# Moving every on-chip pool of a two-layer decoder trunk by 32 bytes

## The chip, the core and the metric

The kernel is one program on one core of a Trainium2 chip. The metric is the device time of that program in microseconds; the comparison is between two programs that compute the same thing from the same inputs. On-chip memory (SBUF) is 128 partitions wide; a tile takes the same byte range in each of them, so an address below is a byte offset within a partition.

## What is computed

A decoder of two layers on 512 tokens of width 1024, all in 4-byte floats. Layer 0 mixes with a gated delta rule (6 heads of 128, worked out in chunks), layer 1 with sliding-window attention (12 query heads, 2 key/value heads); both also attend to 256 memory tokens. After each mixer comes an output product and a gated feed-forward part of width 2816, at the end a norm.

```python
def swiglu(h, w_gate_up, w_down):
    gu = h @ w_gate_up
    return (jax.nn.silu(gu[..., :D_FF]) * gu[..., D_FF:]) @ w_down
...
    for layer in range(DEPTH):
        h = rms_norm(x, ln_mix[layer])
        ...
        x = x + jnp.concatenate([mix_out.astype(x.dtype), mem_o.astype(x.dtype)], axis=-1) @ w_out[layer]
        x = x + swiglu(rms_norm(x, ln_ffn[layer]), w_gate_up[layer], w_down[layer])
    return rms_norm(x, ln_final)
```

Nearly all of the work is in the products with weights: the mixers' input and output products, the two feed-forward parts and the memory keys and values.

## The kernel before

Activations lie transposed: eight tiles of 128 rows (channels) by 512 columns (tokens). A weight arrives by DMA as a raw 128 x 1024 tile (`wraw`); ScalarE copies it to a rounded type (`whi`, type fp32r), VectorE subtracts and keeps the rest (`wlo`). Activations are split in the same way into pairs (`h` and `l`, in the feed-forward part's second half `ac8h` to `ac10l`). A product (`mm3`, called by `project`, `row`, `product` and others) is then three matmuls for each 128 x 128 block: `whi` with the high part, `whi` with the low part, `wlo` with the high part. Line 146 issues all of them; each one also loads its 128 x 128 weights (PEld). Called fp32r matmuls here, they come in two sizes: 512 columns (`pj` tiles most of the time) and 256 columns.

The matmuls with 256 columns come from the feed-forward part: there pairs of gate or up tiles are multiplied by a scheme that saves one block product in eight (`quarters`, `token_sums`); the moving operand is a half of a tile pair `T` (sums of token blocks) or a half of `h` and `l`, the stationary one a half of `whi`/`wlo`. Other matmuls (attention scores, transposes, the delta rule's chunk products, the norm's sums) are in plain float32.

Memory is given out by pools. Pools opened on the left stand one after another upwards from the constants, and stay: `const`, `w` (raw and split weights), `acta`, later `actb` and `x`. Pools with `side="right"` stand downwards from the top, and are opened and closed by stage (`layer0`, `early`, `gdn`, `ffn0`, `swa`, `ffn1`). Each tile's size is rounded up to 32 bytes. `const` holds 3128, 516, 96 and 8 bytes per partition; with the rounding it ends at byte 20320. Here is where the built program puts things:

| operand | pool, side | bytes from a multiple of 128 |
|---|---|---|
| `whi`, `wlo`, `wraw` | w, left | 96 |
| `h`, `l` | acta and actb, left | 96 |
| `x`, `rstd`, `sqa` | x, left | 96 |
| `T`, `ac8h` to `ac10l`, `mh`, `ml`, `mq0h` to `mq1l` | right | 96 |
| other right-hand tiles (`ws`, `fg`, `kn`, `sm`, ...) | right | 0, 32, 64 or 96 |

So of the 6,070 fp32r matmuls 6,042 have both operands at 96; of the rest, 16 (`sc<-h,wabs`, `sc<-l,wabs`) have the moving operand at 96 and the weights at 0, and 12 at the start, on zeros, both at 0.

The order of instructions on each engine follows the order of the calls; a few added dependencies (`nosync`) hold it. TensorE's queue has no DMA issues in it; weights are fetched from SyncE's queue, and the accumulating loads of `quarters` from GpSimd's.

Of the kernel before, what the change touches and what calls it, by code (L numbers as in the profile page):

```python
# [9 lines left out]
F32 = mybir.dt.float32  # L10
# [8 lines left out]
P = 128  # L19
# [67 lines left out]
class Builder:  # L87
# [146 lines left out]
    def build(self):  # L234
        tc, nc, a = self.tc, self.nc, self.a
        with ExitStack() as st:
            opened = lambda name, **kw: tc.tile_pool(name=name, bufs=1, reuse_waits="tile", **kw)
            pool = lambda name, **kw: st.enter_context(opened(name, **kw))
            cp = pool("const")
            self.wpool, self.apool = pool("w"), pool("acta")  # L240
            self.dpool = pool("scratch", space=DRAM)
            self.load_constants(cp)
            self.weng = nc.vector
            with opened("layer0", side="right") as self.mpool:
                with self.banks(pj=3, g=2, sc=3):
                    with opened("early", side="right") as ep:
                        self.mem_and_norm(ep)
                    with opened("gdn", side="right") as gp:
                        mix = self.gdn(gp)
                    self.bpool, xp = pool("actb"), pool("x")  # L250
                    self.x = [self.t(xp, [P, T], F32, f"x{k}") for k in range(KD)]
                    for k in range(KD):
                        nc.sync.dma_start(self.x[k], a["xT"][:, k, :])
                    self.rstd, self.cosT, self.sinT = (self.t(xp, [P, T], F32, n) for n in ("rstd", "cosT", "sinT"))
                    h = self.output(xp, 0, mix)
            with opened("ffn0", side="right") as fp, self.banks(pj=2, g=6):
                self.ffn(fp, xp, 0, h, self.apool, rope=True)
            with self.banks(pj=2, qk=2, pt=2), opened("swa", side="right") as sp:
                h = self.output(xp, 1, *self.swa(sp))
            with opened("ffn1", side="right") as fp, self.banks(pj=2, g=6):  # L260
                self.ffn(fp, xp, 1, h, self.bpool)
# [1154 lines left out]
```

## Time and profile before

| | |
|---|---|
| time, median of 3 runs | 1157.3 us (1157.09 to 1158.04) |
| span of the profiled execution | 1155.8 us |
| mean granted TensorE clock | 0.997 |
| instructions | 19296 |

The profile was taken on one execution of the same program; its span, from the first to the last instruction, is 1.5 us below the median of the timed runs. In its rows a matmul's duration runs from its start to its modelled end, with the time that results take to come out, so durations of neighbours overlap. The pace of a stream is the distance between starts; it is read from the timeline, or from a piece of the chain of waits as its length divided by its count.

### The profile page before, as it was taken

How to read it: one execution, taken by the hardware profiler on the slowest of the kernel's cores; microseconds unless marked ns; L12 is line 12 of the kernel's file. 1: busy time of each engine (PE TensorE's matmuls, PEld its weight loads, DVE VectorE, ACT ScalarE, POOL GpSimd, SP SyncE). 2: the span in 40 equal slices, each digit the busy share in tenths (PEclk: the TensorE clock that was granted, in tenths of full speed). 3: DMA queues.
4: the chain of work that ended last, by engine and by line, in shares of the span. 5: the costliest groups of instructions: out<-in, count | busy, mean ns of one | idle time of the engine just before them, and what ended most of it. 6: DMA issues, size and time to landing. Idle time of an engine off the chain costs nothing.

```text
span 1155.8 us, 19296 instructions
## 1 busy us (share of the span) xinstructions
PE 1142.6 (99%) x7342; PEld 997.1 (86%) x7342; DVE 834.0 (72%) x1559; ACT 626.7 (54%) x1249; POOL 86.0 (7%) x97
## 2 busy tenths in 40 slices
PE   9999999999999999999999999999999999999996
PEld 7788777877899998899998877788899988999886
DVE  5664886767889877488965777839989644889554
ACT  6489672366566642266653554856666412666433
POOL 0230000000101101011100000001111000111000
PEclk9999999999999999999999999999999999999998
DMA  8244341225657636367623421117577533676232
GB/s 314 84 150 116 131 119 66 95 88 164 188 128 182 169 103 168 114 168 187 154 82 99 124 72 42 51 56 200 131 181 184 151 96 107 170 185 153 78 98 85
DMA packets 72559, 151.20 MB, mean 131 GB/s; under 512 B 16732, under 2 KB 18932, under 8 KB 72468
## 3 DMA queue, kind: packets, MB, share of 16 engines
q1 hardware_dynamic: 61060, 129.28, 35.9%
q0 software_dynamic: 11136, 20.45, 11.2%
q8 instruction: 57, 0.93, 0.3%
q14 instruction: 34, 0.28, 0.1%
q10 hardware_dynamic: 272, 0.26, 0.1%
HBM read 143.00 MB, written 6.96 MB: 130 GB/s over the span
## 4 chain that ended last, share of the span: by engine, by line
PE 93%; DVE 3%; ACT 2%; DMA 1%; issue 0%; SPq 0%; DVEq 0%; ACTq 0%
PE pj L146 43%; PE g L146 38%; PE sc L146 6%; PE qk L146 3%; PE pt L146 2%; PE pt L150 1%; PE g L150 1%; DMA wraw<-in_wmk 1%; ACT sm L134 1%; DVE qv L156 1%; DVE big L153 0%; DVE wlo L153 0%; ACT T L140 0%; DVE btmp L153 0%; DMA wraw<-in_wdn 0%
## 5 line engine op out<-in xcount | busy, mean ns | idle before, releaser
L140 ACT ACTIVATE whi<-wraw 128x512 fp32r<-128x512 f32 (+3 forms) x324 | 240.9, 750 | 254.5 <-PE pj L146 159.2
L153 DVE TENSOR_TENSOR wlo<-wraw,whi 128x512 fp32r<-128x512 f32 (+3 forms) x324 | 270.4, 844 | 100.7 <-ACT whi L140 95.2
L146 PE MATMUL pj<-h,whi 128*128 128x512 f32 (+1 forms) x652 | 257.4, 396 | 0.0
L146 PE MATMUL pj<-l,whi 128*128 128x512 f32 (+1 forms) x652 | 255.0, 392 | 0.0
L146 PE MATMUL pj<-h,wlo 128*128 128x512 f32 (+1 forms) x652 | 254.1, 391 | 0.0
L146 PE MATMUL g<-T,whi 128*128 128x256 f32 x1216 | 220.6, 282 | 0.8 <-ACT fs L140 0.8
L146 PEld LDWEIGHTS g<-T,whi 128*128 128x128 f32 x1216 | 186.9, 189 | 2.1 <-DVE fu L156 1.1
L146 PE MATMUL g<-T,wlo 128*128 128x256 f32 x608 | 171.1, 281 | 0.0
L146 PEld LDWEIGHTS pj<-h,whi 128*128 128x128 f32 x652 | 122.4, 188 | 28.6 <-issue 3.6
L146 PE MATMUL g<-h,whi 128*128 128x256 f32 (+1 forms) x500 | 146.5, 293 | 0.0
L146 PE MATMUL g<-h,wlo 128*128 128x256 f32 (+1 forms) x500 | 145.8, 292 | 0.0
L146 PE MATMUL g<-l,whi 128*128 128x256 f32 (+1 forms) x500 | 145.5, 291 | 0.0
L146 PEld LDWEIGHTS pj<-h,wlo 128*128 128x128 f32 x652 | 122.5, 188 | 25.3 <-issue 0.6
L146 PEld LDWEIGHTS pj<-l,whi 128*128 128x128 f32 x652 | 122.6, 188 | 25.2 <-issue 1.1
L146 PEld LDWEIGHTS g<-T,wlo 128*128 128x128 f32 x608 | 114.4, 188 | 0.0
L146 PEld LDWEIGHTS g<-h,whi 128*128 128x128 f32 x500 | 95.0, 190 | 2.3 <-issue 0.5
L146 PEld LDWEIGHTS g<-l,whi 128*128 128x128 f32 x500 | 94.9, 190 | 2.3 <-issue 0.5
L146 PEld LDWEIGHTS g<-h,wlo 128*128 128x128 f32 x500 | 95.0, 190 | 1.7
L1125 POOL DMA_DIRECT2D ws<-in_wgu x38 | 33.3, 875 | 712.5 <-ACT h L140 447.7
L140 ACT ACTIVATE whi<-ws 128x512 fp32r<-128x512 f32 x76 | 48.0, 631 | 49.1 <-PE g L146 41.4
L153 DVE TENSOR_TENSOR fu<-pj,rstd 128x512 f32<-128x512 f32 (+1 forms) x34 | 22.4, 660 | 53.7 <-PE pj L146 53.7
L153 DVE TENSOR_TENSOR wlo<-ws,whi 128x512 fp32r<-128x512 f32 x76 | 52.2, 687 | 7.4 <-ACT whi L140 7.2
(381 smaller groups left out, 1701.1 us busy)
## 6 DMA issues: line engine op xcount, KB each, us to landing
wraw<-in_wgu SPq DMA_DIRECT2D x50, 512.0 KB, 4.2
ws<-in_wgu SPq DMA_DIRECT2D x76, 256.0 KB, 3.6
ws<-in_wgu POOLq DMA_DIRECT2D x76, 256.0 KB, 4.7
wraw<-in_win SPq DMA_DIRECT2D x26, 512.0 KB, 3.6
wraw<-in_wdn SPq DMA_DIRECT2D x32, 384.0 KB, 3.1
wraw<-in_wdn SPq DMA_DIRECT2D x32, 320.0 KB, 3.0
wraw<-in_wgu SPq DMA_DIRECT2D x38, 256.0 KB, 4.3
wraw<-in_wout SPq DMA_DIRECT2D x16, 512.0 KB, 3.6
```

The source lines that it names most:

```text
L134: ins = self.nc.scalar.activation(out, in_, func, **kw).ins
L140: self.copied = self.nc.scalar.activation(out, in_, AF.Copy, **kw).ins
L146: return self.nc.tensor.matmul(out, lhsT, rhs, start=start, stop=stop, skip_group_check=more).ins
L150: return self.nc.tensor.transpose(out, in_, self.ident[:k, :k]).ins
L153: return eng.tensor_tensor(out=out, in0=a, in1=b, op=op).ins
L156: return self.nc.vector.scalar_tensor_tensor(out=out, in0=in0, scalar=scalar, in1=in1, op0=op0, op1=op1).ins
L1125: nc.gpsimd.dma_start(s1, a22, accum_op=ALU.add)
```

## The change

Two tiles of 8 floats (32 bytes) are added that nothing reads or writes, one in a pool behind `const` on the left, and one in a pool opened first on the right.

```diff
             cp = pool("const")
+            self.t(pool("edge"), [P, 8], F32, "edge")
+            self.t(pool("far", side="right"), [P, 8], F32, "far")
             self.wpool, self.apool = pool("w"), pool("acta")
```

Left of it only the constants stay where they were. All other left-hand tiles move up by 32 bytes, all right-hand tiles down by 32. Every engine has the same instructions in the same order with the same waits. The built program's placement of the fp32r matmuls' operands (bytes from a multiple of 128) becomes:

| columns | moving operand | weights | matmuls |
|---|---|---|---|
| 512 | 0 | 0 | 2160 |
| 512 | 0 | 64 (48), 96 (16) | 64 |
| 512 | 64 | 0 | 318 |
| 512 | 96 | 96 (on zeros, at the start) | 12 |
| 256 | 0 | 0 (1416), 64 (144) | 1560 |
| 256 | 64 | 0 (1938), 64 (18) | 1956 |

Right-hand tiles that were at 64 from a multiple of 128 are at 32 now, and those at 0 at 96. Between a left-hand and a right-hand tile the distance is 64 bytes smaller than before.

## The prediction

> **What bounds the kernel now.** I read the page's first two parts, then the chain of waits, then TensorE's own waits, and last the timeline of TensorE inside the chain's longest pieces.
>
> ```profile
> PE 1142.6 (99%) x7342; PEld 997.1 (86%) x7342; DVE 834.0 (72%) x1559; ACT 626.7 (54%) x1249; POOL 86.0 (7%) x97
> PE 93%; DVE 3%; ACT 2%; DMA 1%; issue 0%; SPq 0%; DVEq 0%; ACTq 0%
> PE g L146 <- POOL wabs L366: 1.3, 1, 1.3
> 422.88 65.29 PE pj L146 x285
> 488.16 103.91 PE g L146 x852
> 332.19 88.48 PE g L146 x744
> ```
>
> The first row is the page's busy time, the second its chain, the third the longest entry of TensorE's waits, the last three are pieces of the chain. The reader is to see that TensorE does not wait for anybody: its longest wait in the whole run is 1.3 us, and 93% of the chain that sets the end is its own work. So the time moves when the pace of its matmuls moves, and hardly by anything else. The chain's pieces give that pace: 65.29 / 285 = 229 ns for a stream with mostly 512 columns, 88.48 / 744 = 118.9 ns for one with 256 columns. Now the same at close range, as start, length and count on the timeline:
>
> ```profile
> 460.55 0.40 PE L146 MATMUL pj<-h,whi 128*128 128x512 f32 x1
> ...
> 463.28 0.39 PE L146 MATMUL pj<-h,whi 128*128 128x512 f32 x1
> ...
> 17.22 0.28 PE L146 MATMUL pj<-whi,mh 128*128 128x256 f32 x1
> ...
> 17.82 0.28 PE L146 MATMUL pj<-wlo,mh 128*128 128x256 f32 x1
> ```
>
> From 460.55 to 463.28 there are twelve steps with no gap: 2.73 / 12 = 227.5 ns for 512 columns. The 256-column rows from 17.22 to 17.82 are five steps of 0.12 us, and the long pieces say 118.9 ns. The difference of 256 columns costs 227.5 - 118.9 = 108.6 ns, or 0.424 ns a column. Take the columns away and the same rest is left on both sizes: 227.5 - 512 x 0.424 = 10.4 ns, 118.9 - 256 x 0.424 = 10.4 ns. A rest that does not grow with the size is paid once for each matmul. In columns it is 10.4 / 0.424 = 24.5, which in 4-byte floats is 98 bytes. That is the size of a piece of memory that is read at the start without being needed: with every moving operand at 96 bytes past a multiple of 128 (and 32 past a multiple of 64), a reader that fetches 64 or 128 bytes at a time would need one fetch more than the data has. The rest lies between one such piece of 64 bytes (16 columns, 6.8 ns) and one of 128 (32 columns, 13.6 ns).
>
> **The change, part by part.** It removes and adds no instruction, DMA or wait, and every engine's order is the same. So all of its effect is in how long instructions take at their new addresses. Three kinds have to be looked at.
>
> ScalarE, VectorE and DMAs: nothing. ScalarE's copies of the same size from two places show it:
>
> ```profile
> L140 ACT ACTIVATE whi<-wraw 128x512 fp32r<-128x512 f32 x194 | 120.2, 629 | 70.1 <-PE g L146 49.0 <-PE pj L146 17.3 <-DVE wraw L153 1.8
> L140 ACT ACTIVATE whi<-ws 128x512 fp32r<-128x512 f32 x76 | 48.0, 631 | 49.1 <-PE g L146 41.4 <-ACT fs L140 7.8
> L153 DVE TENSOR_TENSOR wlo<-wraw,whi 128x512 fp32r<-128x512 f32 x194 | 131.1, 690 | 19.8 <-ACT whi L140 14.6
> L153 DVE TENSOR_TENSOR wlo<-ws,whi 128x512 fp32r<-128x512 f32 x76 | 52.2, 687 | 7.4 <-ACT whi L140 7.2
> ```
>
> `wraw` lies at 96, `ws` in most rows at 64: 629 against 631 ns, 690 against 687. Were they to change after all, it is TensorE that hides them (DVE is busy 72%, ACT 54%), and these engines do not end any long wait of TensorE. The transfers are hidden in the same way; a DMA sets 1% of the chain.
>
> Plain float32 matmuls: nothing. The scores of layer 1 give a clean pair, the moving tile `ks` at 0 and `mk` at 96:
>
> ```profile
> L146 PE MATMUL qk<-ks,q x96: 272/376/378, 692.3 to 745.6; 64*128 64x256 f32 x72, 64*128 64x128 f32 x24
> L146 PE MATMUL qk<-mk,q x32: 376/376/480, 665.8 to 680.5; 64*128 64x256 f32 x32
> 16.00 1.03 PE L146 MATMUL g<-sq,consts 128*128 128x256 f32 x4
> ```
>
> Both have a median of 376 ns, so 96 bytes cost plain float32 nothing. But that does not settle it for fp32r. The third row has four float32 rows in 1.03 us; less the last one's own 0.378 us they start 217 ns apart for 256 columns, 0.85 ns a column. That is half the pace of fp32r, so a reader that just keeps up at 0.424 ns a column has slack there, and an extra fetch disappears in it.
>
> The fp32r matmuls: 6,070 of them, and here lies the estimate. No full-speed stream in the trace has its moving operand at a multiple of 64, so the price has to be bounded. At best the rest of 10.4 ns goes, or 13.6 ns if the piece is 128 bytes. At worst nothing is gained (or it is lost, see the third rival). I take the 10.4 ns, since it is measured, for the 512-column ones. For those with 256 columns another floor is near:
>
> ```profile
> 54.33 1.06 PE L146 MATMUL g<-consts,ab 64*128 64x12 f32 x8
> 332.00:421.00 89.00, 89.00 (x748) 88.86 (x746) 77.77 (x139) 54.65 (x105) 11.22 (x13) 1.00 0.66 160
> ```
>
> Eight matmuls with 12 columns have almost nothing to stream, yet take 1.06 us; less the last one's 0.256 us that is 0.80 / 7 = 115 ns for one load of 128 x 128 weights. And in the second row, one stretch of the feed-forward part with its columns span, PE, PEld, DVE, ACT, POOL, the weight loads are busy 88.86 of 89.00 us. So a 256-column matmul comes down from 118.9 to 115 ns and then waits for its weights: 4 ns. The sum, with the counts by place from the table of the change:
>
> - 2,224 with 512 columns, moving operand from 96 to 0: x 10.4 ns = 23.1 us.
> - 1,560 with 256 columns, from 96 to 0: x 4 ns = 6.2 us.
> - Right-hand moving operands go from 96 to 64, which cures a reader of 64 bytes and not one of 128. The rest measured lies between the two, so I take half: 1,956 x 4 / 2 = 3.9 us and 318 x 10.4 / 2 = 1.7 us.
>
> Together 34.9 us. Of the chain 93% is TensorE's, and what is saved where another engine ends a step is not seen: 34.9 x 0.93 = 32.5 us. The profiled span of 1155.8 us becomes 1123; it stands 1.5 us under the median of the timed runs, so the forecast is 1157.3 - 32.5 = **1125 us**. What is late next is the split of weights: in the stretch above VectorE is busy 77.77 of 89.00 us, still 87% after a gain of a few per cent, not full.
>
> The bounds: if the piece is 128 bytes and the 115 ns floor holds, 2,224 x 13.6 + 1,560 x 4 = 36.5 us, x 0.93 = 34 us, 1123 us. If fp32r weights load faster than those of the `ab` rows and all 6,058 full-speed matmuls lose 10.4 ns, it is 63 us, x 0.93 = 59 us, 1099 us. If 64-byte pieces count and each is worth only 6.8 ns, and 4 ns with 256 columns, it is 2,542 x 6.8 + 3,516 x 4 = 31 us, x 0.93 = 29 us, 1128 us.
>
> [...]
>
> **The rivals.**
>
> *Nothing happens.* The rest of 10.4 ns may belong to fp32r itself, as a cost of taking over new weights, or be the reader's rate, and the addresses have no part in it. For it: ScalarE, VectorE and plain float32 do not notice 32 bytes. Against it: the rest has the size of one memory piece, and the pace is not the same everywhere, as the next rows show. The time is then 1157.3 us, with some tenths up or down.
>
> *The pace goes up.* The trace has a case where fp32r matmuls of one size, both operands at 96, are not equally fast:
>
> ```profile
> L146 PE MATMUL pj<-ac9l,whi 128*128 128x512 f32 x30 | 11.9, 398 | 0.0
> L146 PE MATMUL pj<-ac10h,wlo 128*128 128x512 f32 x30 | 11.9, 398 | 0.0
> L146 PE MATMUL pj<-ac8l,whi 128*128 128x512 f32 x30 | 11.6, 387 | 0.0
> L146 PE MATMUL pj<-l,whi x652: 280/389/791, 39.2 to 1140.6; 128*128 128x512 f32 x159, 128*128 128x256 f32 x4
> ```
>
> The right-hand tiles take 387 to 398 ns, a mean of some 394 with their neighbours, where the left-hand `l` has a median of 389. So there is something in the addresses beyond the remainder of 128: reads of the moving operand and of the next weights may meet in the same part of memory. After the change the two start at the same remainder only for left-hand operands, and 2,274 matmuls with a right-hand moving operand have theirs 64 bytes apart. If meeting reads decide, and the 2,224 left-hand matmuls take on the worse pattern, each pays 394 - 389 = 5 to 6 ns: 2,224 x 6 = 13 us, **1170 us**. It decides from the point at which the rest of 10.4 ns stays and the pattern changes; a shorter rest would outweigh it. Against it: left-hand operands and left-hand weights keep their distance to each other.
>
> *The shift cures half.* Only reads at multiples of 128 profit, right-hand tiles at 64 gain nothing or lose what the left gains with 256 columns: 23.1 us x 0.93 = 21 us, 1136 us. This is a smaller form of the forecast and counts with it.
>
> **How the numbers follow.** The forecast and its smaller form, faster by anything from some 12 to 60 us: 0.60. Nothing, within 0.2% (2.3 us, about what a measurement of this kernel can tell from no change): 0.15. Slower by the pattern: 0.25. The likeliest is the forecast, 1125 us, with a range of its own from 1099 to 1145. Below 1102 I leave some 0.05, for the case that nearly all of the rest goes on both sizes. Above it the range has to take in the case of nothing and most of the slower one; above 1168 some 0.12 is left. So the range is 1102 to 1168.
>
> **What would show it.** Right: in the timeline the 512-column steps shrink from 227.5 to 214 to 220 ns, the 256-column steps to about 115; the chain's piece of 285 `pj` matmuls goes from 65.29 to about 62 us, that of 744 `g` matmuls from 88.48 to about 86; ScalarE's and VectorE's rows keep their 629 to 690 ns. If `pj<-h` gains and `pj<-ac8h` and `g<-T` do not, the piece is 128 bytes; if all gain, 64. Wrong: steps of 227.5 and 118.9 ns that stay (nothing), or `pj<-h` rows at 394 ns and more (the pattern). If the pieces shrink but the span does not, other engines have become the bound, which the chain's shares would show.

## The result, and the profile after

The changed kernel takes 1158.12 us (median of 12 runs), the kernel before 1158.27 us (also 12 runs). The ratio is 0.9999, with a 95% interval from 0.999 to 1.0007: no difference that can be measured. The forecast was 1125 us.

The rows that carried the prediction, from the page and the chain of waits of the kernel after:

```profile
PE 1141.8 (99%) x7342; PEld 995.7 (86%) x7342; DVE 834.7 (72%) x1559; ACT 626.7 (54%) x1249; POOL 85.0 (7%) x97
PE 93%; DVE 3%; ACT 2%; DMA 1%; issue 0%; SPq 0%; DVEq 0%; ACTq 0%
422.25 65.33 PE pj L146 x285
487.58 103.88 PE g L146 x852
331.60 88.45 PE g L146 x744
```

The three pieces were 65.29, 103.91 and 88.48 us before: none moved by more than 0.04 us. The timeline of TensorE, at the place that the prediction showed (start, length, count):

```profile
460.62 0.40 PE L146 MATMUL pj<-h,whi 128*128 128x512 f32 x1
...
463.36 0.39 PE L146 MATMUL pj<-h,whi 128*128 128x512 f32 x1
```

Twelve steps in 2.74 us: 228 ns for 512 columns, 227.5 before. The operands do lie at multiples of 128 now, and the step is the same.

Below that the paces did shift, in both directions. The table takes the fp32r matmuls apart by where their operands lie. A step is the distance between the starts of two neighbouring rows of the trace, steps with a wait in them left out, as a mean over the group; the weights are left-hand ones.

| moving operand | columns | matmuls | step before, ns | step after, ns | sum, us |
|---|---|---|---|---|---|
| left | 512 | 2,020 | 228.0 | 228.6 | +1.1 |
| left | 256 | 1,414 | 119.1 | 120.1 | +1.3 |
| right | 512 | 309 | 232.8 | 230.8 | -0.6 |
| right | 256 | 1,915 | 118.8 | 117.8 | -1.9 |

The sums nearly cancel: -0.1 us. So the change is not without effect on the matmuls, but the effect has the size of 0.6 to 1.9 us a group and both signs. Two questions are left: what the rest of some 10 ns in each matmul is, if not a piece of memory read in vain, and what moved these groups.

### The profile page after: what moved, and what is told of

The parts are those of the page before. It is cut to its first block, busy times and chain, and to the rows that moved or that the text cites. A ratio compares the mean times of both kernels' runs of the same rounds, so it can differ in the third digit from the quotient of the medians.

```text
span 1155.9 us, 19296 instructions
## 1 busy us (share of the span) xinstructions
PE 1141.8 (99%) x7342; PEld 995.7 (86%) x7342; DVE 834.7 (72%) x1559; ACT 626.7 (54%) x1249; POOL 85.0 (7%) x97
## 4 chain that ended last, share of the span: by engine, by line
PE 93%; DVE 3%; ACT 2%; DMA 1%; issue 0%; SPq 0%; DVEq 0%; ACTq 0%
PE pj L146 43%; PE g L146 38%; PE sc L146 5%; PE qk L146 3%; PE pt L146 2%; PE pt L150 1%; PE g L150 1%; ACT sm L134 1%; DVE wlo L153 1%; DMA wraw<-in_wmk 1%; DVE qv L156 1%; DVE big L153 0%; ACT T L140 0%; DVE btmp L153 0%; ACT whi L140 0%
```

## The experiments

Two theories stood against each other for the second question. Theory R: each operand's own remainder (its bytes past a multiple of 128) sets its pace, as the prediction had it. Theory D: only the distance between the moving operand and the weights counts.

**A stream at a time.** A kernel of its own ran streams of 24 equal matmuls, on tiles of known place.

```diff
+        m = {o: self.fill(pool, f"m{o}o")[:, o // 4:] for o in (0, 32, 64, 96)}
+        w = {o: self.fill(pool, f"w{o}o", 160)[:, o // 4:o // 4 + P] for o in (0, 32, 64, 96)}
...
+        for o in m:
+            self.run([m[o][:, :T]], [w[0]])
```

> Streams of 24 matmuls each, one after the other on TensorE, nothing else of the model computed (the output is a copy of the input). The step is the distance between starts. Theory A (fetch pieces): fp32r with 512 columns steps at about 216 ns with the moving operand at 0 and at 227 at 32, 64 or 96 bytes past a multiple of 128. Theory B (the rest belongs to fp32r, whatever the address): 227 ns at all four places, 119 or 120 ns for 256 columns at all four, and over 64 to 512 columns a straight line of 0.42 ns a column with a rest of 10 ns above the floor of the weight load (115 ns); plain bf16 without the rest, 215 ns. Theory C (the rest is the price of changing weights or of a stream that meets the weight load): it shrinks with 32 or 64 weight columns in place of 128. Zeros in place of random data cost the same under A, B and C; if they were faster, the rest would be a throttle that depends on data.

The groups of equal shape of that kernel (instructions, busy us, mean ns of one, idle); the number in a tile's name is its remainder (`same` lies at 0), `bfm` is bf16, `c448n` has 448 columns:

```profile
L43 PE MATMUL b<-m0o,w0o 128*128 128x512 f32 x24 | 5.6, 389 | 0.0
L43 PE MATMUL b<-m32o,w0o 128*128 128x512 f32 x24 | 5.8, 395 | 0.0
L43 PE MATMUL b<-same,w64o 128*128 128x512 f32 x24 | 5.8, 394 | 0.0
L43 PE MATMUL b<-bfm,bfw 128*128 128x512 bf16 x24 | 5.3, 379 | 0.0
L43 PE MATMUL b<-c448n,w0o 128*128 128x448 f32 x24 | 5.1, 368 | 0.0
```

In this probe's dense streams a duration is the step plus some 162 ns, so 389 stands for a step of 227 ns and 395 for 233. Theory A falls at the first row: with both operands at 0 the step is 226.7 ns, about the 227.5 of the kernel before with both at 96. Bf16 steps at 215.8 ns, 11 ns less, so most of the rest belongs to fp32r. Weights of 32 columns do not shorten it (231.6 ns), nor do zeros (227.3 ns once the stream has settled). The straight line of theory B holds but for one size: at a granted clock of 1.00 and with both operands at 0, 256, 320, 384 and 512 columns settle at 120.0, 146.7, 173.4 and 226.7 ns, which is 0.4167 ns a column and a rest of 13.3 to 13.4 ns, while 448 columns settle at 206.6, a rest of 20. Its floor of 115 ns does not hold: 64 columns under 128 x 128 weights step at 111.7 ns. And something depends on the addresses after all: with the weights at 0 a moving operand at 32 costs 6 ns more, and weights at 64 under a moving operand at 0 cost as much.

**One side at a time.** The same kernel with only the one or only the other of the two unused tiles.

```diff
-            self.t(pool("far", side="right"), [P, 8], F32, "far")
```

> Only the tile behind the constants: left-hand operands at 0 past a multiple of 128, right-hand ones stay at 96; left and right come 32 bytes nearer instead of 64. Theory R (each operand's own remainder sets its pace): left-hand matmuls as in the changed kernel (512 columns 228.7 ns, 256 columns 119.6), right-hand moving operands as before (118.8 and 232.8). Theory D (the distance between moving operand and weights sets it): left with left as before (228.1 and 119.1), right with left a third value. The time is 1158 us within 2 us under both.

```diff
-            self.t(pool("edge"), [P, 8], F32, "edge")
```

> Only the tile at the top: right-hand operands at 64, left-hand ones stay at 96; left and right again come 32 bytes nearer. Theory R: right-hand moving operands as in the changed kernel (256 columns 117.8 ns, 512 columns 230.8), left-hand ones as before (228.1 and 119.1); that would be some 2 us faster, 1156 us. Theory D: right with left as in the run with the left-hand tile alone, left with left as before.

Each alone is slower: 1162.28 us, a ratio of 1.0033 (1.002 to 1.0046), and 1161.86 us, 1.0032 (1.002 to 1.0045). The two tiles together cost nothing, each by itself 4 us. The pieces of the chain, first with the left-hand tile alone, then with the right-hand one:

```profile
423.46 65.52 PE pj L146 x285
488.98 104.67 PE g L146 x852
```

```profile
423.69 65.52 PE pj L146 x285
489.20 104.67 PE g L146 x852
```

They are equal to 0.01 us, though no remainder is the same in the two: in one the left-hand operands are at 0 and the right-hand ones at 96, in the other at 96 and 64. What they share is the distance, 32 bytes less than before. Right-hand moving operands step at 119.9 and 234.9 ns in both. Theory R is out: it had left them at 118.8 and 232.8 in the first run and brought them to 117.8 and 230.8 in the second. Theory D did not get everything right either: it left the left-hand streams at 119.1 ns with 256 columns, and they step at 119.6 in both runs, for a reason that comes at the end. "1158 us within 2 us" was wrong under both theories; what a distance 32 bytes shorter costs had not been foreseen.

**Distances, and equal remainders.** Streams of 36 on pairs of tiles that all lie alike but for the offsets in their names, `m32w0x` being a moving operand at 32 and weights at 0.

```diff
+        pairs = [(0, 0), (32, 32), (64, 64), (96, 96), (32, 0), (64, 0), (96, 0), (128, 0), (256, 0), (512, 0),
+                 (0, 32), (0, 64), (0, 96), (16, 0), (48, 0)]
```

> Streams of 36 matmuls on tiles that all lie in the same way but for the byte offsets in their names (moving, weights); the model is not computed, the output is a copy of the input. Theory R (each operand's own remainder): the four streams with equal offsets (0 and 0, 32 and 32, 64 and 64, 96 and 96) step differently, the one at 0 fastest. Theory D (only the distance between moving operand and weights counts): those four step alike within 0.5 ns, and 32 or 96 bytes of distance cost some ns with 512 columns; with 64 it is open whether it is as good as 0. Under D streams with 128, 256 and 512 bytes of distance are alike with 0 if the meeting parts are 128 bytes, unlike it if they are larger. bf16 is not touched by 32 bytes under either. The last two streams ask for the rest of 10 to 13 ns: if it is the reader's rate, 128 reads of the same 16 bytes step nearer to 213 ns; if it belongs to the fp32r matmul, they stay at 227.

Groups of equal shape, columns as above:

```profile
L43 PE MATMUL b<-m0w0x,v0w0x 128*128 128x512 f32 x36 | 8.3, 389 | 0.0
L43 PE MATMUL b<-m96w96x,v96w96x 128*128 128x512 f32 x36 | 8.4, 390 | 0.0
L43 PE MATMUL b<-m32w0x,v32w0x 128*128 128x512 f32 x36 | 8.6, 395 | 0.0
L43 PE MATMUL b<-m128w0x,v128w0x 128*128 128x512 f32 x36 | 8.6, 395 | 0.0
L43 PE MATMUL b<-m256w0x,v256w0x 128*128 128x512 f32 x36 | 8.3, 389 | 0.0
L43 PE MATMUL b<-m0w0x,v0w0x 128*128 128x256 f32 x36 | 4.5, 283 | 0.0
L43 PE MATMUL b<-m32w0x,v32w0x 128*128 128x256 f32 x36 | 4.4, 279 | 0.0
```

The four equal offsets are alike: once they have settled all four repeat steps of 227, 227 and 226 ns (three of them start with steps of 224 to 236 ns). At a distance of 128 the step is as long as at 32, at 256 and 512 it is short again, so what counts among these is the distance's remainder by 256. It counts with its sign, as the address of the moving operand less that of the weights: a moving operand 64 bytes above its weights steps at 228.9 ns, one 64 bytes below them (192 by the remainder) at 233.4. And the preference turns with the size: 512 columns are fastest at a distance of 0, 256 columns slowest. The mean steps in ns:

| distance, bytes | 0 | 16 | 32 | 48 | 64 | 96 | 128 | 160 | 192 | 224 | 256 | 512 |
|---|---|---|---|---|---|---|---|---|---|---|---|---|
| 512 columns | 226.7 | 231.8 | 233.3 | 233.4 | 228.9 | 233.7 | 233.5 | 234.0 | 233.4 | 233.2 | 226.8 | 226.7 |
| 256 columns | 119.8 | 116.8 | 116.7 | 118.3 | 117.9 | 119.7 | 118.8 | 117.3 | 117.8 | 118.3 | 119.8 | 120.0 |

The columns of 160, 192 and 224 are the three streams with the weights 96, 64 and 32 bytes above the moving operand.

Now the kernel can be read. There the left-hand activations are at a multiple of 256 from the left-hand weights (20320, 53088 and slices of 512 bytes), the right-hand moving operands (217056, 168928) at 128 past one: the stream has 118.8 ns for that distance and 256 columns, the kernel had 118.8; 233.5 and 232.8 with 512. The change makes the distance 64: 117.9 in the stream and 117.8 in the kernel with 256 columns, 228.9 and 230.8 with 512, where the kernel's streams are nine matmuls long at most. With one tile alone it is 96: 119.7 and 233.7 in the stream, 119.9 and 234.9 in the kernel. bf16 (`bfm`) steps at 215.8 ns in two streams whose distances differ by 32 bytes; it does not notice them.

The same probe gave one hint on the rest: reading the same 16 bytes 128 times as moving operand, the step was 219 ns.

**Everything shifted, distances kept.**

```diff
-        g = self.t(cp, [P, G_N], F32, "gains")
+        both = self.t(cp, [P, G_N + 7], F32, "gains")
+        g = both[:, :G_N]
...
-        v = self.t(cp, [P, 2], F32, "eps")
+        v = both[:, G_N + 1:G_N + 3]
...
+            self.t(pool("far", side="right"), [P, 8], F32, "far")
```

> Every tile on both sides lies 32 bytes lower than before (the small tile eps moved into the spare columns of gains, and the unused tile on the right kept), so all fp32r operands are at 64 past a multiple of 128 and every distance between left and right is that of the kernel before. Theory D: each stream of fp32r matmuls keeps the pace of before to 0.1 ns (228.0 and 232.8 with 512 columns, 119.1 and 118.8 with 256), the time is 1158 us. Theory R: the paces move, since 96 became 64, by an amount that the theory cannot tell.

1157.82 us, ratio 1.0 (0.9991 to 1.0009). The chain's pieces:

```profile
422.80 65.27 PE pj L146 x285
488.07 103.91 PE g L146 x852
```

They and the piece of 744 (88.48 us) are the pieces of before to 0.02 us, and the four groups step at 228.0, 232.8, 119.1 and 118.8 ns. All 6,042 pairs went from 96 to 64 past a multiple of 128, and no change of pace or time followed from it.

**96 bytes at the top.**

```diff
+            self.t(pool("far", side="right"), [P, 24], F32, "far")
```

> Only the tile at the top, with 96 bytes: right-hand operands at a multiple of 128, left-hand ones at 96, left and right 96 bytes nearer. Theory D with parts of 64 bytes: 96 is as bad as 32, so right-hand moving operands step at 119.9 ns and 234.9 ns as in the runs with one tile of 32 bytes, and the time is some 4 us longer, 1162 us. Theory R: right-hand moving operands gain, as far as a multiple of 128 is better than one of 64, and the time falls to 1155 us or less.

1158.71 us, ratio 1.0001 (0.9992 to 1.001). Here theory D had been given too short a period, 64 bytes. By the period of 256 the distance is 128 - 96 = 32: the stream has 116.7 and 233.3 ns, the kernel showed 118.0 and 233.5. Both forecasts of the time were wrong. The expectation was written before the second probe had shown the table.

**The rest.** Streams at a distance of 0, with one of the two reads made light.

```diff
+        same = lambda t, n, k=4: t[:, 0:k].unsqueeze(1).to_broadcast([P, n // k, k])
...
+                if name in ("wsame", "both"):
+                    w = b[:, 0:1].to_broadcast([P, P])
+                if name in ("msame", "both"):
+                    m = same(a, n)
+                if name == "mline":
+                    m = same(a, n, 64)
```

> Streams of 36 matmuls as before (the model is not computed), all with moving operand and weights at a distance that is a multiple of 256 bytes. One of the two reads is made light: weights of 64 or 32 columns, weights that are one column read 128 times, moving columns that are the same 16 bytes, or the same 256 bytes, again and again, and both at once. Theory E (the rest of 13 ns with 512 columns is the two reads meeting): it goes away with either read made light, to 214 to 216 ns, and both together add nothing. Theory F (the rest is the reader of the moving operand alone, which cannot keep 4 bytes a column at full clock): only the light moving reads help (219 ns was seen), weights of 32 columns leave 227. Theory G (the rest is the fp32r matmul's own): 227 everywhere but for the 219 seen.

Groups of equal shape; `mw` with 128*32 has 32 weight columns, with 128*64 it has 64; `mmline` reads the same 256 bytes, `mmsame` the same 16:

```profile
L46 PE MATMUL b<-mfull,vfull 128*128 128x512 f32 x36 | 8.3, 389 | 0.0
L46 PE MATMUL b<-mw,vw 128*32 128x512 f32 x36 | 8.5, 394 | 0.0
L46 PE MATMUL b<-mmline,vmline 128*128 128x512 f32 x36 | 8.3, 389 | 0.0
L46 PE MATMUL b<-mmsame,vmsame 128*128 128x512 f32 x36 | 8.0, 381 | 0.0
L46 PE MATMUL b<-mfull,vfull 128*128 128x256 f32 x36 | 4.5, 283 | 0.0
L46 PE MATMUL b<-mw,vw 128*64 128x256 f32 x36 | 4.3, 276 | 0.0
L46 PE MATMUL b<-mmsame,vmsame 128*128 128x256 f32 x36 | 4.2, 274 | 0.0
```

With 512 columns a lighter weight read does not help, it even costs 3 to 5 ns (230.0 ns with 64 columns, 231.7 with 32, 231.1 with one column read 128 times); reading the same 16 bytes as moving operand saves 8 ns (a step of 218.7), and making the weights light as well adds nothing (218.7). Reading the same 256 bytes saves nothing. That is nearest to theory F, though F had light weights at 227: most of the rest goes with the reading of the moving operand. With 256 columns either read made light shortens the step, from 120.0 to 111.9 ns with the same 16 bytes and to 113.3 with 64 weight columns (117.8 with 32, 116.7 with one column), and both at once add nothing (111.9), which is nearer to theory E. So no theory of the three covers both sizes. What separates 218.7 from bf16's 215.8 ns stays open, and so does what in the reading takes the time.

**Distances set on purpose.** First the right-hand tiles of the feed-forward part 128 bytes lower. The small tile `minus` moves into spare columns of `gains`; the other lines, which stand alike for the second layer, are:

```diff
-            with opened("ffn0", side="right") as fp, self.banks(pj=2, g=6):
+            with opened("padffn0", side="right") as q, opened("ffn0", side="right") as fp, self.banks(pj=2, g=6):
+                self.t(q, [P, 32], F32, "padffn0")
```

> The right-hand tiles of the feed-forward part lie 128 bytes lower and nothing else moves (the small tile minus went into the spare columns of gains to make room): T and the ac tiles come to a distance from the weights that is a multiple of 256 bytes. Theory D with a period of 256 bytes, by the second probe's steps: right-hand moving operands with 512 columns go from 232.8 to 227 ns, with 256 columns from 118.8 to 119.8, left-hand ones with 512 columns from 228.0 to 227 since no stream before them is out of step. That is 318 x 5.8 + 2,022 x 1.0 less 1,914 x 1.0 = 2 us faster, 1156 us. If the period were 64 or 128 bytes nothing moves.

1159.13 us, ratio 1.001 (1.0001 to 1.0019). The chain's pieces:

```profile
423.51 64.63 PE pj L146 x285
488.14 104.79 PE g L146 x852
```

The streams that were moved did what was expected: 227.3 ns with 512 columns (expected 227) and 119.95 with 256 (expected 119.8). The time was not: left-hand matmuls with 512 columns gained 0.35 ns, not 1.0, and those with 256 columns, whose distance did not change, went from 119.1 to 120.0, which costs 1.2 us that the forecast did not have. Then only T, by 96 bytes:

```diff
+        if j == 1:
+            self.t(fp, [P, 24], F32, "padT")
         g0, g1 = (self.gain(G_FFN[layer], j + i) for i in (0, 4))
```

> Only the tiles below the ac tiles on the right in the feed-forward part lie 96 bytes lower, T among them: T comes to 32 bytes of distance from the weights, where the second probe has its shortest step with 256 columns (116.7 ns), and the ac tiles stay. Theory D: right-hand moving operands with 256 columns go from 118.8 to between 116.7 and 118.0 ns (the latter is what the run with 96 bytes at the top showed), those with 512 columns stay at 232.8; 1,824 x 0.8 to 2.1 = 1.5 to 4 us faster, less up to 1 us that the left-hand streams may lose behind them: 1155 to 1157 us.

1157.51 us, ratio 0.9997 (0.9988 to 1.0006). T steps at 118.1 ns, the upper end of what was expected, the right-hand tiles with 512 columns at 232.8 as expected, and left-hand matmuls with 256 columns at 119.7 against 119.1. The gain of a piece of 852 is 0.15 us; the time cannot be told from that of before.

**Both at their own distance.** T at 32, the ac tiles at 0.

```diff
+        for n in range(KD, half):
+            self.pair(fp, f"ac{n}")
...
-            with opened("ffn0", side="right") as fp, self.banks(pj=2, g=6):
+            with opened("padffn0", side="right") as q, opened("ffn0", side="right") as fp, self.banks(pj=2, g=6):
+                self.t(q, [P, 24], F32, "padffn0")
```

The same lines stand for the second layer.

> Both kinds of right-hand operand at the distance that suits them, in the feed-forward part alone: the ac tiles (512 columns) at a multiple of 256 bytes from the weights, T (256 columns) at 32 bytes. The ac tiles are given their place first, and an unused tile of 96 bytes stands above the pool. Theory D, by the pieces of the chain in the two runs that moved one kind each: the pieces of 285 pj matmuls come to 64.6 us (65.3 before), those of 852 g matmuls to 103.8 (103.9 before), together 2.9 us less, so 1155.0 us, a ratio of 0.9975, if no transfer at the start of the feed-forward part comes later for its new place. If the two gains spoil each other (the pace carries over from one stream to the next), the pj pieces stay near 65 us and the time near 1157.

1155.47 us against 1158.25, ratio 0.9975 (0.9966 to 0.9984), as expected, and faster than both kernels of the case. The chain's pieces, of the first layer:

```profile
487.79 103.76 PE g L146 x852
423.14 64.65 PE pj L146 x285
```

## Why the prediction was wrong

*What bounds the kernel* was right: TensorE's pace. The chain is 93% TensorE's in both kernels, and each run above that changed the time did so in the chain's pieces of TensorE.

*ScalarE, VectorE, transfers and plain float32 at nothing* was right as far as it can be seen: VectorE's busy time is 834.0 and 834.7 us, ScalarE's 626.7 twice, and `qk<-ks` and `qk<-mk` keep their median of 376 ns. The pair that was to show it was none: in the built program `ws` lies at 96 in all 76 rows, as `wraw` does. What shows it is the same rows after the change, with all of these tiles moved by 32 bytes: `whi<-wraw` 629 ns in both kernels, `whi<-ws` 631 and 630, `wlo<-wraw,whi` 690 and 689.

*The step that failed* is the one that made a rest into a place in memory: 10.4 ns a matmul, or 98 bytes, read "at the start without being needed", since every moving operand stood at 96 past a multiple of 128. With the operands at 0 the step was 228 ns in the kernel (227.5 before) and 226.7 in the stream. The size of the rest was no evidence for it. Streams with both operands at 0, 32, 64 and 96 step alike, and shifting all of the kernel by 32 bytes with the distances kept changes none of the pieces shown by more than 0.02 us. The row that could have warned was there: the float32 pair `ks` and `mk`, at 0 and 96 and alike. It was set aside with the argument that float32 has slack; for fp32r an operand's own remainder turned out to matter as little (228.0 ns in the left-hand streams with 512 columns at 96 and at 64).

*The rest that does not grow with the size* was a line through two points, 227.5 ns from a stream that had not settled and 118.9 from a mixture of streams. In the probe four sizes from 256 to 512 columns lie on such a line, at 0.4167 ns a column, with a rest of 13.3 to 13.4 ns; 448 columns have 20. So a rest of about this size is there, but it stands at every remainder alike and is mostly fp32r's own: bf16, with 215.8 ns for 512 columns and 109.2 for 256 in the first probe, has 2.5 ns by the same working. With 512 columns 8 ns of it go with the moving operand's reading (226.7 against 218.7 in the third probe).

*The sum* fell with that step: a gain of 23.1 us for left-hand operands with 512 columns was a loss of 1.1, one of 6.2 us with 256 columns a loss of 1.3. The floor of 115 ns for a weight load, which made 10.4 ns into 4 for the 256-column ones, does not hold either: 128 x 128 fp32r weights step at 111.9 ns in the third probe where the moving operand is light to read, and at 111.7 in the first with 64 columns. The row that it was read from has plain float32 weights on 64 partitions.

*Right-hand operands at 64* were given half. They did gain, 1.0 ns a matmul with 256 columns and 2.0 with 512, for another reason: their distance from the weights went from 128 to 64 past a multiple of 256.

*The rival that nothing happens* gave the time, and half of its reason: the rest does belong for the most part to fp32r (226.7 ns with 512 columns against bf16's 215.8). The other half, that the addresses have no part in it, is wrong; the time came out equal because 2.4 us lost and 2.5 us gained cancel, and that they do is luck.

*The rival that the pace goes up* named the right quantity, the distance between the two operands (that their reads meet in one part of memory is not shown), and was given the wrong price: it moved the left-hand operands into the worse pattern, which keep their distance. With a change of 32 in the distance instead of 64, the time does go up, by 4 us rather than 13, and the right-hand operands pay most of it. That both tiles were shifted, and by the same amount towards each other, is what made the sum nothing: the distance of 64 is good for right-hand operands, and the left-hand streams next to them lose as much.

Why left-hand streams change when only their neighbours' distance does can be placed, by the starts in the traces, but not explained. From the ninth matmul of a stream on, left-hand matmuls with 256 columns step at 120.0 ns in every run of the kernel, as in the probe at a distance of 0. All of the difference lies in the first eight, nearly always behind a right-hand stream. Their mean is 118.1 ns before, 120.2 with both tiles, 119.1 with either alone and 119.9 with the right-hand tiles 128 bytes lower. So the pace of a stream carries over some eight matmuls into the next one. What in the chip carries it stays open, and so does why the distance counts at all.

## What to carry to other kernels

A rest in the pace of matmuls is not yet a reason; measure a stream at two places before a sum is built on it, and take the row that already shows no effect seriously. For fp32r matmuls look at the distance between moving operand and weights by 256 bytes, not at each operand's alignment: here 512 columns wanted 0 and right-hand operands with 256 columns 32, which was worth 0.25%. And a shift of one side of the memory plan by 32 bytes cost 0.3%, so when a small edit moves tiles, compare the pace of streams that it does not touch.

## What the runs showed of the hardware that was not expected

- In the second probe the step of fp32r matmuls depends on the distance from the weights to the moving operand, with a period of 256 bytes among the distances tried: with 512 columns 226.7 ns at 0, 256 and 512, 229 at 64, 232 to 234 at 16, 32, 48, 96, 128, 160, 192 and 224. For 256 columns it is 120 ns at 0 and 116.7 at 32.
- In the kernel's runs a stream keeps something of the one before it for some eight matmuls: left-hand fp32r matmuls with 256 columns step at 118.1 to 120.2 ns on average there, by the distance of their neighbours, and at 120.0 from then on.
- fp32r with 512 columns steps 11 ns longer than bf16 (226.7 against 215.8 in the first two probes) at each remainder tried with moving operand and weights alike (0, 32, 64 and 96), their distance a multiple of 256.
- In the third probe a moving operand of 16 bytes read again and again steps at 218.7 ns with 512 columns, one of 256 bytes at 226.7. Weights that are light to read make the step 3 to 5 ns longer with 512 columns, at a distance of 0, and 2 to 7 ns shorter with 256.
